# A first stage that takes x laid out transposed, in a two-layer trunk of mLSTM and retention heads

## The chip, the cores and the metric

The kernel runs on one core of a Trainium2 chip. The metric is device time in microseconds, from the start of the program to its end on that core; smaller is better. The core has five engines that run their own instruction streams in order and wait for each other by semaphores: TensorE (PE in the profile, with its weight loads listed apart as PEld), VectorE (DVE), ScalarE (ACT), GpSimd (POOL) and SyncE (SP), which here issues the transfers. TensorE reads SBUF and writes PSUM, which has eight banks of 128 partitions by 512 float32 in this kernel's use.

## The reference

Two layers; x is 1024 tokens by 1024 channels, float32. Each layer is

```
shift, scale, gate = split(silu(c) @ w_ada + b_ada, 3)          # one row each, from the condition c
h = x * rsqrt(mean(x*x, over channels) + eps) * norm_g * (1 + scale) + shift
p = h @ w_in                                                    # 1024 x 9224: gates and q, k, v of two head groups
y = concat(mLSTM heads(p), retention heads(p))                  # 4 + 4 heads of 256
x = x + gate * (y @ w_out)
```

and at the end stands one more root-mean-square norm of x. Only `h` of the first layer is computed in a different way by the change. To form it one needs, for each token, the root over its channels, and for each channel a gain `norm_g * (1 + scale)` and a shift, which come from c and a third of w_ada (two of its three column blocks; 8 MB).

## The kernel before, in words

The projections want `h` transposed: channels on partitions (eight blocks k of 128 channels), tokens along the free axis (two halves of 512). Each such tile `hT[k][half]` is kept as a pair of float32r tiles, a high part and a low part (`h` minus its high part), and each product is three matmuls: weight high by h high, weight high by h low, weight low by h high (`mm3`, lines 145 to 147).

The first stage (everything ahead of the call of `head_cols` for layer 0) makes `hT` for layer 0 and, as tiles become ready, multiplies them with the first three weight blocks (`first`, called F). It is set out by hand: a string of steps in the program, `script`, is walked in order, and each step appends its instructions to the queues of the engines it uses. No planner reorders them; within an engine the order of the string is the order of execution. The steps before are:

- the prologue: c is loaded, then eight tiles of w_ada (group 0, `ada_load`, L236), x of half 0 (L1061, eight tiles of 128 tokens by 512 channels), the first half of three weight blocks (L1076), x of half 1, w_ada groups 1 and 2, the second half of the weights, w_ada group 3, some small rows. Each tile has 256 KB. All go through SP's queue.
- `S`, `Q`, `R`: squares of x with a running sum along the free axis, half on ACT (L1072), half on DVE (L1069), then the root of each token by POOL's power (L1013), a column per 128 tokens.
- `N`, `X`: x times its token's root, a column operand (L308 on ACT, L310 on DVE).
- `A g a b`: DVE multiplies the tiles a to b of w_ada's group g with c and adds them up (L244, then L246): one group yields gain and shift of two channel blocks.
- `P g`: four one-column matmuls sum the group over its partitions (L251). `G g`: three small DVE operations turn that into gain and shift (L227, L229, L230).
- `T n`: four 128 by 128 transposes on TensorE bring one channel block of one half to PSUM (L315). `n` counts the sixteen pieces in the order: blocks 0 and 1 of half 0, blocks 0 and 1 of half 1, blocks 2 and 3 of half 0, and so on.
- `E n`: gain and shift while the block leaves PSUM (L321 on ACT, L323 on DVE). `C n`: high part (ACT, L1137). `U n`: low part (DVE, L1140).
- `F n`: nine matmuls of 512 columns, three weight blocks times high and low.
- `W i p`: a raw weight tile is split into high and low; the low part on POOL or DVE (L614, L615). `V n`: a piece of the v weights, split by ACT and POOL.
- `D n`: n matmuls on a constant (L1151).

Behind the last F comes a transpose of parameter rows (`head_cols`, L206) and then the v projection, and from there on the stages of layer 0 and 1, whose order on the other engines is chosen by a scheduler and on TensorE is fixed by the program.

Of the kernel before, what the change touches and what calls it, by code (L numbers as in the profile page):

```python
# [19 lines left out]
P = 128  # L20
# [59 lines left out]
@with_exitstack  # L80
def tile_hybrid_trunk(ctx, tc, x, c, positions, w_ada, b_ada, norm_g, w_in, conv_w, conv_b,
                      b_igate, b_fgate, gn_m, gn_r, w_out, final_g, consts, out):
# [477 lines left out]
    def ocol(hg, m):  # L560
        return OFF_MO + hg * HD + m * P
# [493 lines left out]

    def load_x(half):
        xt = [[bt() for _ in range(2)] for _ in range(4)]
        for tt in range(4):
            row = half * 4 + tt
            for cc in range(2):  # L1060
                Q.dma_start(xt[tt][cc], x[row * P:(row + 1) * P, cc * 512:(cc + 1) * 512])  # L1061
        return xt

    def squares(xt, ss, rows):
        for tt in rows:
            for cc in range(2):
                o = wt("th", 512, 5)
                if cc:
                    V.scalar_tensor_tensor(o, xt[tt][cc], 1.0, xt[tt][cc], ALU.mult, ALU.mult,  # L1069
                                           accum_out=ss[:, tt, cc:cc + 1])  # L1070
                else:
                    A.activation(o, xt[tt][cc], AF.Square, accum_out=ss[:, tt, cc:cc + 1])  # L1072

# [5 lines left out]

    xss = [new_ss(), new_ss()]  # L1080
# [12 lines left out]
    araw.append(ada_load(0, 3))  # L1093
    vgr = v0_gates(0)
# [4 lines left out]
    ada_cols(0, arows)  # L1099
    accs = [bt()]  # L1100
    ada_group(araw[0], accs[0], range(KT))
    pad = ps_a()

    for l in range(DEPTH):
# [7 lines left out]

        def first(half, k):
            for i, w in enumerate(wf):
                if k == 0:
                    pf[i][half] = ps_p() if i < 2 else ps_a()
                half_block(pf[i][half], w, hT, half, k, k + 1)

        if l == 0:
            seq = [(half, k) for g in range(4) for half in range(2) for k in (2 * g, 2 * g + 1)]  # L1120
            w0, pts, hfs, rs1 = [], {}, {}, []
            script = ("P0 D6 S G0 W00 W10 N0 W20 T0 T1 E0 E1 C0 C1 U0 U1 F0 F1 Q R A102 X0 A124 T2 E2 C2 A146 T3 D3 E3 C3 U2 F2 "
# [4 lines left out]
            for step in script.split():  # L1127
                what, arg = step[0], step[1:]
                n = int(arg) if arg.isdigit() else 0
                if what == "T":  # L1130
                    pts[n] = norm_transpose(xts[seq[n][0]], seq[n][1])
                elif what == "E":
                    hfs[n] = norm_evac(0, pts.pop(n), seq[n][1], n >= 2)
                elif what == "C":
                    half, k = seq[n]
                    hT[k][half] = (bt(F32R), bt(F32R))
                    A.copy(hT[k][half][0], hfs[n])  # L1137
                elif what == "U":
                    half, k = seq[n]
                    V.tensor_tensor(hT[k][half][1], hfs.pop(n), f(hT[k][half][0]), ALU.subtract)  # L1140
                elif what == "F":
                    first(*seq[n])
                elif what == "A":
                    g, a, b = (int(d) for d in arg)
                    if len(accs) == g:
                        accs.append(bt())
                    ada_group(araw[g], accs[g], range(a, b))
                elif what == "D":
                    warm = ps_a()
                    for i in range(n):  # L1150
                        PE.matmul(warm[:, 0:256], rmask[:, 0:P], rmask[:, 0:256], start=True, stop=True)  # L1151
                elif what == "P":
                    ada_sums(0, n, accs[n], pad)
                elif what == "G":
                    finish_gsh(0, 2 * n, 2, pad[:, 4 * n:4 * n + 2], pad[:, 4 * n + 2:4 * n + 4])
                elif what == "Q":
                    squares(xts[1], xss[1], range(4))
                elif what == "R":
                    rs1 = row_rstd(xss[1], "nrm")
                elif what == "S":  # L1160
                    squares(xts[0], xss[0], range(4))
                    rs0 = row_rstd(xss[0], "nrm")
                elif what == "N":
                    if n == 0:
                        norm_scale(xts[0], rs0, (0,), (0, 2))
                    else:
                        norm_scale(xts[0], rs0, (1,), range(4), range(2 * n - 2, 2 * n))
                elif what == "X":
                    if n == 0:
                        norm_scale(xts[1], rs1, (0,), (0, 2))  # L1170
                    else:
                        norm_scale(xts[1], rs1, (1,), range(4), range(2 * n - 2, 2 * n))
                elif what == "V":
                    w0.append(v0_split(vgr, vrw[n], n))
                    if n + 4 < KT:
                        vrw.append(v0_raw(0, n + 4))
                else:
                    i, p = (int(d) for d in arg)
                    wf[i] += split_w(rw[i][p], P, V if p else G)
# [89 lines left out]

_INS = ['x', 'c', 'positions', 'w_ada', 'b_ada', 'norm_g', 'w_in', 'conv_w', 'conv_b', 'b_igate', 'b_fgate',  # L1270
        'gn_m', 'gn_r', 'w_out', 'final_g']
# [25 lines left out]
```

## Time and profile before

| | us |
|---|---|
| median of 3 runs | 2311.9 (2310.84 to 2314.16) |
| the profiled execution | 2311.88 |
| its span, first to last instruction | 2310.0 |
| TensorE busy in the span | 2277.8 |
| start of the first F in the profile | 24.41 |
| start of L206 behind the last F | 73.96 |

A row of the timeline reads: start, duration, engine, line, operation, output and inputs by name, shapes, how many were merged into the row; in square brackets, the idle time of the engine just before it and what ended that. Where several were merged, the duration runs from the first start to the last end. A row of the table by windows has the stretch, its length, then for each engine the busy time and the number of instructions, then the clock that TensorE was granted as a share of full speed, the busy share of the transfer engines and GB/s. The chain of waits is followed back from the last instruction; in order of time its rows are start, duration, and what was being waited for or done.

### The profile page before, as it was taken

The page shows a single profiled execution, that of the slowest core. Times are in us where ns is not written, and L with a number is a line of the kernel's source. Part 1 is how long each engine was busy: PE and PEld are TensorE (multiplying, and loading weights), DVE is VectorE, ACT ScalarE, POOL GpSimd, SP SyncE. Part 2 cuts the span into 40 slices and gives each one's busy share as a digit, 9 for nine tenths or more (in the row PEclk, how much of TensorE's full clock was granted, in tenths as well). Part 3 has the DMA queues.
Part 4 walks back from the last instruction along what each step waited for, and adds up shares of the span by engine and source line. Part 5 has one row for each costly group of instructions (what it writes and reads, how often), then busy time and mean ns, then how long its engine had stood idle before and what let it go on. Part 6 is the DMA issues. An engine that isn't in the chain of part 4 may idle for free.

```text
span 2310.0 us, 34281 instructions
## 1 busy us (share of the span) xinstructions
PE 2277.8 (99%) x12447; PEld 1958.2 (85%) x12447; DVE 1353.2 (59%) x2835; ACT 907.1 (39%) x1768; POOL 823.5 (36%) x817
## 2 busy tenths in 40 slices
PE   7999999999999999999999999999999999999998
PEld 5888888889988888888888889888898888988886
DVE  7477688556555555584536665555563545556753
ACT  5535433444332323353434544344443323224442
POOL 1343424333343334222552434233334334341323
PEclk9999999999999999999999999999999999999999
DMA  8223232324433533486532322322323333436762
GB/s 257 80 64 98 73 84 80 82 74 116 120 109 88 150 83 87 128 258 217 177 92 57 84 72 77 84 74 69 81 70 89 81 87 93 124 81 205 240 231 78
DMA packets 328761, 259.44 MB, mean 112 GB/s; under 512 B 79732, under 2 KB 263804, under 8 KB 328592
## 3 DMA queue, kind: packets, MB, share of 16 engines
q1 hardware_dynamic: 328592, 257.27, 38.6%
q8 instruction: 97, 1.59, 0.3%
q14 instruction: 72, 0.59, 0.1%
HBM read 201.58 MB, written 55.61 MB: 111 GB/s over the span
## 4 chain that ended last, share of the span: by engine, by line
PE 91%; DVE 3%; DMA 3%; issue 1%; POOL 1%; ACT 1%; SPq 0%; POOLq 0%; DVEq 0%; ACTq 0%
PE pp L145 24%; PE pp L146 24%; PE pp L147 24%; PE pa L146 5%; PE pa L147 5%; PE pa L145 5%; PE pa L765 2%; DMA b<-in_w_ada_dram 1%; DMA b<-in_x_dram 1%; PE pa L315 0%; DMA raw<-in_w_ada_dram 0%; POOL wL L615 0%; POOL sL L615 0%; DVE b L266 0%; DMA b<-in_w_in_dram 0%
## 5 line engine op out<-in xcount | busy, mean ns | idle before, releaser
L145 PE MATMUL pp<-b,wH 128*128 128x512 f32 x1776 | 703.7, 396 | 1.1 <-ACT b L1137 1.1
L146 PE MATMUL pp<-b,wH 128*128 128x512 f32 x1776 | 700.2, 394 | 0.3 <-DVE b L1140 0.2
L147 PE MATMUL pp<-b,wL 128*128 128x512 f32 x1776 | 700.2, 394 | 0.0
L615 POOL TENSOR_TENSOR wL<-raw,wH 128x512 fp32r<-128x512 f32 x338 | 450.1, 1338 | 507.4 <-ACT wH L614 466.8
L147 PEld LDWEIGHTS pp<-b,wL 128*128 128x128 f32 x1776 | 333.9, 188 | 79.0
L146 PEld LDWEIGHTS pp<-b,wH 128*128 128x128 f32 x1776 | 334.2, 188 | 72.2 <-DVE b L1140 2.0
L145 PEld LDWEIGHTS pp<-b,wH 128*128 128x128 f32 x1776 | 334.4, 188 | 71.5 <-ACT b L1137 1.6
L614 ACT CAST wH<-raw 128x512 fp32r<-128x512 f32 x402 | 246.1, 616 | 322.8 <-PE pp L147 93.8
L145 PE MATMUL pp<-wH,b 128*128 128x256 f32 (+1 forms) x1152 | 353.0, 306 | 0.7 <-DVE g L543 0.7
L147 PE MATMUL pp<-wH,b 128*128 128x256 f32 (+1 forms) x1152 | 352.8, 306 | 0.0
L146 PE MATMUL pp<-wL,b 128*128 128x256 f32 (+1 forms) x1152 | 352.2, 306 | 0.0
L615 POOL TENSOR_TENSOR b<-acc,b 128x256 fp32r<-128x256 f32 (+1 forms) x208 | 200.8, 984 | 322.8 <-ACT b L614 315.2
L145 PEld LDWEIGHTS pp<-wH,b 128*128 128x128 f32 x1152 | 216.9, 188 | 12.3 <-DVE g L543 1.6
L147 PEld LDWEIGHTS pp<-wH,b 128*128 128x128 f32 x1152 | 216.6, 188 | 11.4
L146 PEld LDWEIGHTS pp<-wL,b 128*128 128x128 f32 x1152 | 216.7, 188 | 10.8
L632 DVE SCALAR_TENSOR_TENSOR acc<-pp,cols,acc 128x511 f32<-128x511 f32 (+2 forms) x192 | 142.5, 742 | 43.2 <-ACT acc L627 41.2
L614 ACT CAST b<-acc 128x256 fp32r<-128x256 f32 (+1 forms) x208 | 93.7, 487 | 187.4 <-DVE acc L709 127.6
L615 POOL TENSOR_TENSOR sL<-th,sH 128x384 fp32r<-128x384 f32 (+1 forms) x64 | 61.0, 953 | 236.5 <-ACT sH L614 171.9
L145 PE MATMUL pa<-wH,b 128*128 128x512 f32 x256 | 101.1, 395 | 0.0
L147 PE MATMUL pa<-wH,b 128*128 128x512 f32 x256 | 101.0, 394 | 0.0
L146 PE MATMUL pa<-wL,b 128*128 128x512 f32 x256 | 100.9, 394 | 0.0
L636 ACT ACTIVATE th<-acc 128x512 f32<-128x512 f32 x64 | 40.5, 632 | 146.3 <-DVE acc L634 79.3
(255 smaller groups left out, 3439.3 us busy)
## 6 DMA issues: line engine op xcount, KB each, us to landing
raw<-in_w_in_dram SPq DMA_DIRECT2D x274, 256.0 KB
raw<-in_w_out_dram SPq DMA_DIRECT2D x128, 256.0 KB
gdr<-g SPq DMA_DIRECT2D x64, 256.0 KB
ndr<-zt SPq DMA_DIRECT2D x128, 128.0 KB
raw<-in_w_ada_dram SPq DMA_DIRECT2D x64, 256.0 KB
g<-gdr SPq DMA_DIRECT2D x64, 256.0 KB
acc<-ndr SPq DMA_DIRECT2D x64, 256.0 KB
acc<-kdr SPq DMA_DIRECT2D x192, 64.0 KB
```

Of the source, the lines that this page charges most:

```text
L145: PE.matmul(o, lt[0], rt[0], start=start, stop=False)
L146: PE.matmul(o, lt[0], rt[1], start=False, stop=False)
L147: PE.matmul(o, lt[1], rt[0], start=False, stop=stop)
L614: A.copy(dst[0], src)
L615: eng.tensor_tensor(dst[1], src, f(dst[0]), ALU.subtract)
L632: V.scalar_tensor_tensor(acc[:, d:], pt[:, 0:HALF - d], wcol, acc[:, d:], ALU.mult, ALU.add)
L636: A.activation(th, acc, AF.Tanh, scale=0.5)
L765: PE.matmul(pd, kk[i][:, o:o + P], qd, start=dt == 0 and i == 0, stop=dt == 1 and i == 1)
```

## The change

The program gets a second copy of x, transposed (`xt`, channels by tokens), as an input; the first stage loads that, sixteen tiles of 128 channels by 512 tokens, and loads all of it ahead of everything but a few rows. The untransposed x is still read later for the residual. No transposes are left in the first stage, and a piece is now a tile of xt.

Since channels lie on partitions, the sum of squares of a token runs over partitions. New steps: `Z n`: ACT squares tile n (0 to 7 half 0, 8 to 15 half 1). `M n`: four matmuls with a 128 by 128 block of the squares as weights and a column of ones, each into its own bank, summed over the eight tiles of a half. `B`: four small DVE operations (L1077) and POOL's power (L1078) give the roots, token on partition. `I`/`J`: the roots times an identity, four diagonals side by side, on DVE (half 0) or POOL (half 1) (L1082). `O`: one float32 matmul of 512 columns with ones spreads them over all partitions (L1087). `R`: ACT copies that to SBUF (L1167). `X n`/`Y n`: tile n times the spread roots, on DVE or POOL (L1170). `H`: high part straight from gain and shift on ACT (L1173); `E`: the same result in full, in place (L1175); `U`/`L`: low part on DVE or POOL (L1177). `F` has its six matmuls with high parts first, then the three with low parts; this order holds in the second layer's first block too (L1131, L1132, L1134). `D n` is two matmuls that read tile n (from 16 on, a tile of w_ada's group 0). In a split, a small `w` puts the low part on DVE, a capital `W` on POOL.

```diff
-            script = ("P0 D6 S G0 W00 W10 N0 W20 T0 T1 E0 E1 C0 C1 U0 U1 F0 F1 Q R A102 X0 A124 T2 E2 C2 A146 T3 D3 E3 C3 U2 F2 "
-                      "A168 U3 P1 G1 N1 T4 F3 E4 C4 U4 N2 A202 T5 F4 E5 C5 U5 X1 A224 T6 F5 E6 C6 U6 X2 A246 T7 F6 E7 C7 "
-                      "A268 U7 W01 W11 W21 P2 G2 T8 F7 E8 C8 A302 U8 T9 F8 E9 C9 A324 U9 T10 F9 E10 C10 A346 U10 T11 F10 "
-                      "E11 C11 A368 U11 P3 G3 T12 F11 E12 C12 U12 T13 F12 V0 E13 C13 V1 U13 T14 F13 E14 C14 V2 U14 "
-                      "T15 F14 E15 C15 V3 U15 V4 F15 V5 V6 V7")
+            script = ("Z0 M0 Z1 M1 Z2 M2 Z3 M3 Z4 M4 Z5 M5 Z6 M6 Z7 M7 B0 Z8 M8 Z9 M9 I0 Z10 M10 Z11 M11 Z12 M12 O0 "
+                      "Z13 M13 Z14 M14 Z15 R0 M15 Y0 A001 B1 J1 A013 D17 D18 O1 R1 Y1 A035 D20 Y2 A057 A078 P0 w00 "
+                      "W10 G0 w20 H0 E0 A102 U0 F0 H1 E1 Y8 L1 Y9 F1 H2 E2 H3 E3 A124 L2 F2 Y3 A148 P1 G1 L3 F3 w21 "
+                      "H4 E4 H5 E5 X10 X11 L4 F4 A203 L5 W01 H6 E6 L6 W11 H7 E7 F5 A236 F6 A268 X4 P2 G2 L7 F7 H8 E8 "
+                      "Y5 H9 E9 X12 X13 L8 F8 A304 H10 E10 L9 F9 H11 E11 A348 Y6 L10 F10 P3 G3 L11 F11 H12 E12 Y7 "
+                      "U12 X14 F12 H13 E13 U13 F13 X15 H14 E14 L14 F14 V0 V1 H15 E15 U15 F15 V2 V3 V4 V5 V6 V7")
...
+    def token_squares(t):
+        o = wt("th", 512, 5)
+        A.activation(o, t, AF.Square)
+        return o
+
+    def token_sums(pt, o, start, stop):
+        for i in range(4):
+            PE.matmul(pt[i][:, 0:1], o[:, i * P:(i + 1) * P], ones, start=start, stop=stop)
+
+    def token_rstd(pt):
+        s = cst.tile([P, 4], F32, tag="nrm", bufs=2, name=nm("s"))
+        rs = cst.tile([P, 4], F32, tag="nrmr", bufs=2, name=nm("rs"))
+        for i in range(4):
+            V.tensor_scalar(s[:, i:i + 1], pt[i][:, 0:1], 1.0 / D, EPS, ALU.mult, ALU.add)
+        G.tensor_tensor(rs, s, mhalf, ALU.pow)
+        return rs
+
+    def spread_diag(dg, rs, eng=V):
+        eng.tensor_tensor(dg.rearrange("p (a b) -> p a b", a=4), ident.unsqueeze(1).to_broadcast([P, 4, P]),
+                        rs.unsqueeze(2).to_broadcast([P, 4, P]), ALU.mult)
+
+    def spread(dg):
+        pt = ps_a()
+        PE.matmul(pt, f(ones_r), dg, start=True, stop=True)
+        return pt
...
+    xh = [load_xt(half) for half in range(2)]
+    firsts = (zcol(0, 0), ocol(0, 0), zcol(0, 1))
     araw = [ada_load(0, 0)]
-    xts = [load_x(0)]
-    firsts = (zcol(0, 0), ocol(0, 0), zcol(0, 1))
     rw = [[w_raw(col, 0)] for col in firsts]
-    xts.append(load_x(1))
     araw.append(ada_load(0, 1))
-    araw.append(ada_load(0, 2))
     for i, col in enumerate(firsts):
         rw[i].append(w_raw(col, 1))
+    araw.append(ada_load(0, 2))
     araw.append(ada_load(0, 3))
...
         def first(half, k):
+            hH, hL = hT[k][half]
             for i, w in enumerate(wf):
                 if k == 0:
                     pf[i][half] = ps_p() if i < 2 else ps_a()
-                half_block(pf[i][half], w, hT, half, k, k + 1)
+                PE.matmul(pf[i][half], w[k][0], hH, start=k == 0, stop=False)
+                PE.matmul(pf[i][half], w[k][1], hH, start=False, stop=False)
+            for i, w in enumerate(wf):
+                PE.matmul(pf[i][half], w[k][0], hL, start=False, stop=k == KT - 1)
...
+                elif what in "XY":
+                    t = xh[n // 8][n % 8]
+                    (V if what == "X" else G).tensor_tensor(t, t, R[n // 8], ALU.mult)
+                elif what == "H":
+                    hT[k][half] = (bt(F32R), bt(F32R))
+                    A.activation(hT[k][half][0], src, AF.Identity, scale=gain, bias=shift)
                 elif what == "E":
-                    hfs[n] = norm_evac(0, pts.pop(n), seq[n][1], n >= 2)
+                    A.activation(src, src, AF.Identity, scale=gain, bias=shift)
+                elif what in "UL":
+                    (V if what == "U" else G).tensor_tensor(hT[k][half][1], src, f(hT[k][half][0]), ALU.subtract)
...
+                    t = xh[n // 8][n % 8] if n < 16 else araw[0][n - 16]
+                    for i in range(2):
+                        PE.matmul(warm[:, 0:256], rmask[:, 0:P], t[:, 0:256], start=True, stop=True)
```

More of the change, by code (lines that the diff above doesn't have):

```diff
@@ L1054, in tile_hybrid_trunk, with load_xt @@
     hT = [[None, None] for _ in range(KT)]
[L1056 to L1072, printed above, removed]
+    def load_xt(half):
+        tiles = []
+        for k in range(KT):
+            t = bt()
+            Q.dma_start(t, xt[k * P:(k + 1) * P, half * HALF:(half + 1) * HALF])
+            tiles.append(t)
+        return tiles
+    def token_squares(t):
[19 more added lines that the diff above has]
+        return pt
     def w_raw(col, p):
@@ L1078, in w_raw @@
         return raw
-    xss = [new_ss(), new_ss()]
     crow = wt("rows", P, 2)
@@ L1099, in tile_hybrid_trunk @@
     ada_cols(0, arows)
-    accs = [bt()]
-    ada_group(araw[0], accs[0], range(KT))
+    accs = []
     pad = ps_a()
@@ L1129, in tile_hybrid_trunk @@
                 n = int(arg) if arg.isdigit() else 0
-                if what == "T":
-                    pts[n] = norm_transpose(xts[seq[n][0]], seq[n][1])
-                elif what == "E":
-                    hfs[n] = norm_evac(0, pts.pop(n), seq[n][1], n >= 2)
[L1134 to L1140, printed above, removed]
+                if what in "HEULF":
+                    half, k = seq[n]
+                    src = xh[half][k]
+                    gain, shift = gsh[0][:, 0, k:k + 1], gsh[0][:, 1, k:k + 1]
+                if what == "Z":
+                    sqs[n] = token_squares(xh[n // 8][n % 8])
+                elif what == "M":
+                    if n % 8 == 0:
+                        sums[n // 8] = [ps_p() for _ in range(4)]
+                    token_sums(sums[n // 8], sqs.pop(n), n % 8 == 0, n % 8 == 7)
+                elif what == "B":
+                    rss[n] = token_rstd(sums[n])
+                elif what in "IJ":
+                    spread_diag(dg[n], rss[n], V if what == "I" else G)
+                elif what == "O":
+                    prs[n] = spread(dg[n])
+                elif what == "R":
+                    A.copy(R[n], prs[n])
+                elif what in "XY":
[4 more added lines that the diff above has]
+                    A.activation(hT[k][half][0], src, AF.Identity, scale=gain, bias=shift)
+                elif what == "E":
+                    A.activation(src, src, AF.Identity, scale=gain, bias=shift)
+                elif what in "UL":
+                    (V if what == "U" else G).tensor_tensor(hT[k][half][1], src, f(hT[k][half][0]), ALU.subtract)
                 elif what == "F":
-                    first(*seq[n])
+                    first(half, k)
                 elif what == "A":
```

31 lines of the change are left out of this document (7 added, 24 removed).

## The prediction

> **What bounds the kernel now.** I read the page's engine shares first, then the chain of waits, then the first 80 us on the timeline, because the change touches nothing later.
>
> ```profile
> span 2310.0 us, 34281 instructions
> PE 2277.8 (99%) x12447; PEld 1958.2 (85%) x12447; DVE 1353.2 (59%) x2835; ACT 907.1 (39%) x1768; POOL 823.5 (36%) x817
> ...
> PE 91%; DVE 3%; DMA 3%; issue 1%; POOL 1%; ACT 1%; SPq 0%; POOLq 0%; DVEq 0%; ACTq 0%
> ```
>
> TensorE carries the chain. Behind the first stage the instructions of every engine are the same in both programs, apart from a few neighbours swapped, so a later end of the first stage is a later end of the kernel. The stage's end in PE's order is the transpose of the head's rows (L206), whose start I take as the mark.
>
> ```profile
> 73.72 0.40 PE L147 MATMUL pa<-b,wL 128*128 128x512 f32 x1
> 73.96 0.25 PE L206 MATMUL pa<-ident,rows 96*128 96x96 f32 x1
> ```
>
> Up to that mark, where does the stage wait? The chain in order of time says: on transfers until 46, then on TensorE.
>
> ```profile
> 38.83 7.19 DMA b<-in_w_ada_dram
> 46.06 1.94 DMA rows<-in_conv_w_dram
> ```
>
> The weights of the conditioning arrive last. Both programs load the same 54 tiles of 256 KB through the same queue, so I let that end stay at 46 and cost the SP queue at nothing in total; only the order inside it moves. Landings read off the engines that waited for them:
>
> ```profile
> 5.08 0.49 DVE L244 TENSOR_SCALAR b<-b,cact 128x512 f32<-128x512 f32 x1 [0.96 <-DMA b<-in_w_ada_dram]
> ...
> 11.92 0.75 DVE L246 SCALAR_TENSOR_TENSOR b<-b,cact,b 128x512 f32<-128x512 f32 x1 [0.19 <-DMA b<-in_w_ada_dram]
> ```
>
> ```profile
> 12.47 0.63 ACT L1072 ACTIVATE th<-b 128x512 f32<-128x512 f32 x1 [9.25 <-DMA b<-in_x_dram]
> ...
> 18.09 0.62 ACT L614 CAST wH<-b 128x512 fp32r<-128x512 f32 x1 [0.84 <-DMA b<-in_w_in_dram]
> ```
>
> Tile 1 lands at 5.1, tile 8 at 11.9, tile 17 at 18.1. So all of x is there by about 17.5 in the new order, and the first conditioning group, tiles 17 to 24, by 18.1 + 7 x 0.75 = 23.4 (256 KB at the 350 GB/s of the windows below).
>
> **Part 1, the sums of squares on TensorE (Z, M, B, I/J, O, R).** Removed are 64 transposes. Added are 16 x 4 matmuls that load a 128x128 block of squares and move one column, the form of L251. They are f32, and the trace shows an f32 matmul as two records (L251 issues four, the row says x8; the six warm-up matmuls of L1151 are x12).
>
> ```profile
> 12.73 1.86 PE L251 MATMUL pa<-ones,b 128*128 128x1 f32 x8 [8.90 <-DVE b L246]
> ...
> 14.46 5.47 PE L1151 MATMUL pa<-rmask 128*128 128x256 f32 x12
> ...
> 24.41 0.79 PE L145 MATMUL pp<-b,wH 128*128 128x512 f32 x1 [1.12 <-ACT b L1137]
> ...
> 30.55 0.40 PE L147 MATMUL pp<-b,wL 128*128 128x512 f32 x1
> 30.79 0.39 PE L145 MATMUL pa<-b,wH 128*128 128x512 f32 x1
> ...
> 31.48 1.06 PE L315 MATMUL pa<-ident,b 128*128 128x128 f32 x8
> ...
> 36.80 0.95 PE L251 MATMUL pa<-ones,b 128*128 128x1 f32 x8
> 37.61 0.63 PE L315 MATMUL pa<-ident,b 128*128 128x128 f32 x4
> ```
>
> Removed: 64 x 1.06/8 = 8 us of TensorE. Added: 128 records. At 12.73 eight take 14.46 - 12.73 = 1.73 (0.216 each); at 36.80 eight take 37.61 - 36.80 = 0.81 (0.101 each). The sums cost 27.7 or 13.0, by the clock. Which?
>
> ```profile
> 13.41:16.83 3.42, 3.42 (x12) 2.97 (x13) 1.81 (x6) 1.75 (x5) 0.00 (x0) 1.00 1.07 385
> 16.83:20.24 3.41, 3.09 (x8) 1.92 (x6) 2.00 (x8) 2.28 (x6) 1.73 (x2) 1.00 1.13 334
> 20.24:23.65 3.41, 1.53 (x8) 0.87 (x8) 2.99 (x4) 1.17 (x3) 3.35 (x3) 0.96 1.05 393
> 23.65:27.07 3.42, 2.66 (x6) 1.84 (x7) 3.39 (x9) 3.23 (x9) 0.00 (x0) 0.50 1.08 366
> 27.07:30.48 3.41, 3.41 (x10) 2.69 (x9) 2.86 (x9) 0.68 (x3) 1.19 (x1) 0.54 1.10 350
> ```
>
> These windows (length, then busy time and count of PE, PEld, DVE, ACT, POOL, then granted clock) are cut where the clock changes: full from 20.24, half from 23.65, full from 30.48. Before 20.24 no clock is recorded and the column shows 1.00; the pitch, 0.456 a record in the warm-up, shows half speed. In 13.41 to 16.83 PE was busy throughout, 1 us of it with one-column sums, and the clock stayed low; one window filled almost wholly with wide matmuls (16.83 to 20.24, and again 27.07 to 30.48) raised it. I take it that one-column sums don't count as work, and price all of them at 0.216. The other reading, that the rise comes one window late whatever fills it, stays as a rival.
>
> The Trainium skill, "TensorE: Matmul & The Clock Gate", section "Part 1: The HAM clock gate", states that about 4 us of sustained matmul activity lift the array to full clock. By that, the sums, unbroken from 5.8, would be at full clock from about 10; the two rises here came 6 us after the first wide matmul, and no row shows sums alone.
>
> Place by place: the first square ends at 5.1 + 0.6; the sums run from 5.8 without a break, since 1.73 a piece is slower than the landings; the roots of half 0 (four small reads of the banks that the next sums need) add 0.5 (0.16 each, as L227 below); the spreading product O0 stands among the sums and is f32 of 512 columns, 4 x 0.456 = 1.8. The last sum ends at 5.8 + 27.7 + 0.5 + 1.8 = 35.8. B1 on DVE waits for it, and behind B1 in DVE's order are seven of the eight multiply-adds of the first conditioning group, whose data landed long before. After B1: 36.3. The warm-ups D17, D18, D20 (4 x 0.456 each) and O1 follow on PE until 35.8 + 7.3 = 43.1 and are covered by what comes next on DVE.
>
> **Part 2, the moves to POOL.** The scaling by the token root becomes 16 products of two tensors (7 on DVE, 9 on POOL); of the 16 low parts 12 go to POOL; three weight splits and one diagonal are there too. That is 25 operations of 128x512 with two SBUF inputs on POOL, where this stage had 3 (and the small v splits at its end). What does such an operation do to a DVE one with two SBUF inputs?
>
> ```profile
> 19.50 4.09 POOL L615 TENSOR_TENSOR wL<-b,wH 128x512 fp32r<-128x512 f32 x3
> ```
>
> ```profile
> 563.11 1.29 POOL L615 TENSOR_TENSOR wL<-raw,wH 128x512 fp32r<-128x512 f32 x1
> 563.29 1.65 DVE L266 SCALAR_TENSOR_TENSOR b<-raw,cact,b 128x512 f32<-128x512 f32 x1 [0.64 <-DMA raw<-in_w_ada_dram]
> ...
> 564.35 1.74 POOL L615 TENSOR_TENSOR wL<-raw,wH 128x512 fp32r<-128x512 f32 x1
> 564.98 1.67 DVE L266 SCALAR_TENSOR_TENSOR b<-raw,cact,b 128x512 f32<-128x512 f32 x1
> ```
>
> ```profile
> 28.88 0.48 DVE L244 TENSOR_SCALAR b<-b,cact 128x512 f32<-128x512 f32 x1
> 29.39 0.75 DVE L246 SCALAR_TENSOR_TENSOR b<-b,cact,b 128x512 f32<-128x512 f32 x1
> ...
> 31.07 3.11 DVE L246 SCALAR_TENSOR_TENSOR b<-b,cact,b 128x512 f32<-128x512 f32 x4
> ...
> 37.78 0.16 DVE L227 TENSOR_TENSOR gsh<-pa,cols 128x2 f32<-128x2 f32 x1 [0.94 <-PE pa L251]
> ...
> 38.04 0.16 DVE L230 TENSOR_TENSOR gsh<-sm,cols 128x2 f32<-128x2 f32 x1
> ...
> 49.12 1.89 DVE L615 TENSOR_TENSOR wL<-b,wH 128x512 fp32r<-128x512 f32 x3
> ```
>
> They take turns. Alone the DVE form takes 0.75, four of them 3.11 (pitch 0.79); beside POOL each ends 0.55 after the POOL operation does (563.11 + 1.29 = 564.40, DVE ends at 564.94), and the POOL operation after it is held as well (1.74). POOL ends at 564.40 and 566.09, so a pair takes 1.69, and a POOL operation that meets a busy DVE costs DVE 1.69 - 0.79 = 0.9. The bounds are 0 (POOL always elsewhere in time) and 1.29 (the whole operation).
>
> The Trainium skill, "SBUF — State Buffer", section "SBUF: two separate sides", states that the port pair shared by DVE and GpSimd is an exclusive lock held for the whole instruction. The trace agrees that they alternate; taken at the full 1.29 for 23 operations the sum would be 23 x 0.39 = 9 us more.
>
> DVE's order has, per conditioning group: eight multiply-adds, then G waits for P on PE, which waits for the eighth, and the next group stands behind G. From the rows: P and G together are 38.20 - 36.80 + 0.1 = 1.5. DVE's own work between G's, at pitches of 0.60 (a split, a low part or a product, as the three at 49.12), 0.51 (L244, 28.88 to 29.39) and 0.79 (L246), and the POOL operations that meet it by the two orders:
> - to P0: 7 x 0.79 = 5.5, and dg1, Y1, Y2, W10, Y8: 5 x 0.9. From 36.3: 46.3.
> - G0 to G1: 2 x 0.60 + 0.51 + 7 x 0.79 = 7.2, and L1, Y9, L2, Y3, L3: 4.5. With 1.5: 13.2.
> - G1 to G2: 3 x 0.60 + 6.0 = 7.8, and L4, L5, W01, L6, W11, L7, Y5: 6.3. With 1.5: 15.6.
> - G2 to G3: 2 x 0.60 + 6.0 = 7.2, and L8, L9, Y6, L10, L11, Y7: 5.4. With 1.5: 14.1.
>
> P0 follows a pause of PE, so I take its slow row: 46.3 + 1.86 + 0.55 = 48.7 for G0. F0 starts one H (below) later, at 49.4 (24.41 before). G3: 48.7 + 13.2 + 15.6 + 14.1 = 91.6. TensorE needs 36 x 0.232 + 0.8 = 9.2 a group and is not the limit there: it waits at P1, P2 and P3, where P stands ahead of an F that could run.
>
> **Part 3, behind G3.** F11 stands behind P3 (done at 91.2), then F12 to F15: 45 matmuls at 0.232 (30.79 after 30.55, rounded) are 10.4. PE paused for some 4 us before P3, so it may restart at half clock (0.43) for one or two windows: 1.7 to 3.4, taken as 2.5. U12 and U15 add 0.5. Mark: 104.6, against 73.96: +31.
>
> Edits at nothing. ACT's H and E:
>
> ```profile
> 39.63 1.33 ACT L308 ACTIVATE b<-b,rs 128x512 f32<-128x512 f32 x2
> ```
>
> Two are 1.33, so a piece's pair is done before POOL's part for the piece ahead (1.69); without that cover, at most one piece, 1.3. POOL's splits of the v weights follow L14 and feed the product behind the mark: 0 to 2.5 late, kept in the range. In the second layer the low parts come after the high ones, 64 records swapped; TensorE is busy throughout there, so nothing.
>
> Sum: 2311.9 + 31 = 2343; the profiled execution took 2311.9 (span 2310.0), which is the median of the runs.
>
> **The rivals.**
> (a) The sums do raise the clock. For: the late-rise reading of 13.41 to 20.24, and the skill's rule. Then they end at 5.8 + 3 x 1.73 + 13 x 0.81 + 0.5 + 0.9 = 22.9 (three pieces slow), everything behind is 12.9 earlier: mark at 92, +18, 2330.
> (b) DVE and POOL don't collide, the sums are slow. For: POOL waits for ACT often. Against: by both orders POOL has work ready in each group. DVE is done at 41.8, PE's warm-ups at 43.1, P0 and G0 2.4 and H: F0 at 46.2, then 144 x 0.232 + 3 x 0.8 + 2.5: mark at 84.5, +10, 2322.
> (c) Faster: TensorE is again the only limit of the stage, with 8 us of transposes and pauses gone. It decides from F0 at 38 on, since 144 x 0.232 + 3 x 0.8 = 36 lie between it and the mark: earlier is faster. With F0 at 31 (sums as in (a), B1 0.5, first group 5.5, P0 to F0 2.1): 67, -7, 2305. For: DMA allows it, the first group lands at 23.4. Against: the 0.216 and the 1.69.
>
> **How the numbers follow.** (The runs tell no change from about 0.2%, 4.6 us.) Forecast 0.46, (a) 0.25, (b) 0.12, (c) 0.12, within 0.2% (between (b) and (c)) 0.05. Slower 0.83, same 0.05, faster 0.12. Alone the forecast lies in 2336 to 2350 (collisions at 0.7 to 1.1 each, restart 1.7 to 3.4, v splits up to 2.5). The range leaves out (c) and no change below, and the top: 2317 to 2348.
>
> **What would show it.** Right: sums at 0.21 a record, the last near 36; B1 followed by an unbroken run of L246 at 1.7 apart beside POOL; F0 near 49; PE idle ahead of P1, P2, P3 with DVE L246 as releaser. Wrong: sums at 0.10 with the clock full by 13; L246 at 0.75 while POOL runs; PE without a pause from F0 on; or ada3 landing later than 46.

## The result and the profile after

The changed kernel took 2340.25 us (median of 4 runs, 2338.49 to 2341.04) against 2311.66 (4 runs): a ratio of 1.0121, 95% interval 1.0103 to 1.0138. It is slower by 28.6 us; the forecast was 2343. The profiled execution took 2340.62, its span is 28.9 longer. The page of the changed kernel:

```profile
span 2338.9 us, 34415 instructions
PE 2303.9 (99%) x12509; PEld 1982.9 (85%) x12509; DVE 1358.6 (58%) x2813; ACT 908.6 (39%) x1760; POOL 858.8 (37%) x839
```

The shares hardly tell the two kernels apart; the first 102 us do. The timeline of TensorE in the changed kernel (start, duration, line, operation, operands, records, and in brackets the idle time ahead and what ended it):

```profile
5.61 22.35 PE L1071 MATMUL pp<-ones,th 128*128 128x1 f32 x104 [1.73 <-ACT th L1066]
27.82 2.05 PE L1087 MATMUL pa<-g,ones_r 128*128 128x512 f32 x2
29.67 5.12 PE L1071 MATMUL pp<-ones,th 128*128 128x1 f32 x24
34.65 3.76 PE L1189 MATMUL pa<-b,rmask 128*128 128x256 f32 x8
...
43.85 1.84 PE L251 MATMUL pa<-ones,b 128*128 128x1 f32 x8 [2.98 <-DVE b L246]
47.11 0.80 PE L1131 MATMUL pp<-b,wH 128*128 128x512 f32 x1 [1.42 <-ACT b L1173]
...
56.90 1.05 PE L251 MATMUL pa<-ones,b 128*128 128x1 f32 x8 [0.44 <-DVE b L246]
...
72.51 1.87 PE L251 MATMUL pa<-ones,b 128*128 128x1 f32 x8 [4.60 <-DVE b L246]
...
87.46 1.87 PE L251 MATMUL pa<-ones,b 128*128 128x1 f32 x8 [2.94 <-DVE b L246]
...
102.11 0.25 PE L206 MATMUL pa<-ident,rows 96*128 96x96 f32 x1
```

The sums (L1071), with the spreading product O0 (L1087) among them, hold TensorE without a break until 34.8; F0 (the first L1131) starts at 47.11 (24.41 before); TensorE waits for VectorE's multiply-adds (L246) ahead of all four P (L251); the mark, L206, is at 102.11, 28.15 later than the 73.96 of before. All but half a us of the 28.6 stands ahead of the mark.

VectorE and GpSimd in the changed kernel, from the same timeline; L230 ends a G:

```profile
34.91 8.80 DVE L246 SCALAR_TENSOR_TENSOR b<-b,cact,b 128x512 f32<-128x512 f32 x7
...
45.99 0.16 DVE L230 TENSOR_TENSOR gsh<-sm,cols 128x2 f32<-128x2 f32 x1
...
58.26 0.16 DVE L230 TENSOR_TENSOR gsh<-sm,cols 128x2 f32<-128x2 f32 x1
...
60.67 11.79 DVE L246 SCALAR_TENSOR_TENSOR b<-b,cact,b 128x512 f32<-128x512 f32 x7
63.44 1.76 POOL L615 TENSOR_TENSOR wL<-b,wH 128x512 fp32r<-128x512 f32 x1
65.14 1.75 POOL L1177 TENSOR_TENSOR b<-b,b 128x512 fp32r<-128x512 f32 x1
66.85 1.72 POOL L615 TENSOR_TENSOR wL<-b,wH 128x512 fp32r<-128x512 f32 x1
...
74.68 0.16 DVE L230 TENSOR_TENSOR gsh<-sm,cols 128x2 f32<-128x2 f32 x1
...
89.62 0.16 DVE L230 TENSOR_TENSOR gsh<-sm,cols 128x2 f32<-128x2 f32 x1
```

Seven multiply-adds take 11.79, 1.68 each, while GpSimd's operations start 1.70 apart. Alone they take 0.75. The two engines take turns, as forecast.

In the runs below the mark moves by what the stage gains or loses. It is read in the one execution that was profiled, and the total is the median of all; against the kernel before, the median moved between 2 us less and 5 us more than the mark. So mechanisms are read at the mark, the totals stand beside it, and a total that hits its forecast within 5 us shows little by itself. All in us; the ratio is to the kernel before:

| kernel | F0 | G3 done | mark | median | ratio (95%) |
|---|---|---|---|---|---|
| before | 24.41 | 62.04 | 73.96 | 2311.66 | |
| changed | 47.11 | 89.78 | 102.11 | 2340.25 | 1.0121 (1.0103 to 1.0138) |
| all on VectorE | 47.85 | 85.20 | 95.17 | 2336.93 | 1.0108 (1.0093 to 1.0123) |
| first group first | 44.89 | 89.89 | 101.48 | 2342.14 | 1.0131 (1.0116 to 1.0146) |
| one record a sum | 35.75 | 78.44 | 90.72 | 2327.28 | 1.0066 (1.0049 to 1.0083) |
| warm-ups first | 47.45 | 89.30 | 100.91 | 2343.35 | 1.0133 (1.0118 to 1.0148) |
| first group free | 38.38 | 84.14 | 94.17 | 2335.40 | 1.0099 (1.0085 to 1.0113) |
| before, x first | 34.08 | 72.76 | 84.63 | 2320.58 | 1.0036 (1.0022 to 1.0049) |
| rearranged | 29.48 | 62.88 | 72.87 | 2312.41 | 1.0002 (0.9992 to 1.0011) |
| two tiles on TensorE | 29.11 | 65.52 | 75.87 | 2315.43 | 1.0012 (1.0003 to 1.0021) |
| rearranged, full sums | 40.35 | 73.72 | 83.69 | 2323.44 | 1.0050 (1.0032 to 1.0068) |

### The profile page after: what moved, and what is told of

The parts are those of the page before. It is cut to its first block, busy times and chain, and to the rows that moved or that the text cites. A ratio compares the mean times of both kernels' runs of the same rounds, so it can differ in the third digit from the quotient of the medians.

```text
span 2338.9 us, 34415 instructions
## 1 busy us (share of the span) xinstructions
PE 2303.9 (99%) x12509; PEld 1982.9 (85%) x12509; DVE 1358.6 (58%) x2813; ACT 908.6 (39%) x1760; POOL 858.8 (37%) x839
## 5 line engine op out<-in xcount | busy, mean ns | idle before, releaser
L146 PE MATMUL pp<-b,wH 128*128 128x512 f32 x1712 | 675.0, 394 | 0.0
L145 PE MATMUL pp<-b,wH 128*128 128x512 f32 x1712 | 674.5, 394 | 0.0
L147 PE MATMUL pp<-b,wL 128*128 128x512 f32 x1712 | 674.5, 394 | 0.0
L147 PEld LDWEIGHTS pp<-b,wL 128*128 128x128 f32 x1712 | 321.5, 188 | 75.1
L145 PEld LDWEIGHTS pp<-b,wH 128*128 128x128 f32 x1712 | 321.7, 188 | 68.5
L146 PEld LDWEIGHTS pp<-b,wH 128*128 128x128 f32 x1712 | 321.6, 188 | 68.2
L146 PEld LDWEIGHTS pp<-wL,b 128*128 128x128 f32 x1152 | 216.7, 188 | 10.7
```

Source lines behind the costliest of these rows:

```text
L145: PE.matmul(o, lt[0], rt[0], start=start, stop=False)
L146: PE.matmul(o, lt[0], rt[1], start=False, stop=False)
L147: PE.matmul(o, lt[1], rt[0], start=False, stop=stop)
```

## The experiments

**All products and low parts on VectorE: do the two engines collide?** The letters Y, L and J of the order (GpSimd) become X, U and I (VectorE), at the same places.

```diff
-"... M15 Y0 A001 B1 J1 A013 ... Y8 L1 Y9 F1 ... Y6 L10 F10 P3 G3 L11 F11 ..."
+"... M15 X0 A001 B1 I1 A013 ... X8 U1 X9 F1 ... X6 U10 F10 P3 G3 U11 F11 ..."
```

> The 9 products, 12 low parts and one diagonal that the change gave to GpSimd go to VectorE, at the same places of the order; only three weight splits stay on GpSimd. Theory (each GpSimd operation with two SBUF inputs costs a busy VectorE 0.9 us, since the two take turns): each of the 22 costs VectorE 0.60 instead of 0.9. Ahead of G0 four of them are in the way, between G0 and G1 five, G1 and G2 five, G2 and G3 six: G0 1.2 earlier (44.5), G0 to G1 10.8 (12.3 in the changed kernel), G1 to G2 14.9 (16.4), G2 to G3 13.1 (14.9); together 6 us, 2334. Rival (the two do not collide, VectorE is slow there for another reason): VectorE gets 22 x 0.60 = 13 us more to do, 2353. A multiply-add that stands with none of the three splits beside it takes 0.79 by the theory, still over 1.2 by the rival.

The mark came 6.9 earlier (95.17). The groups by line and form, of the changed kernel between 60.6 and 72.5 us and of this one between 50 and 85 (after the bar: busy us, mean ns of one, idle us ahead):

```profile
L246 DVE SCALAR_TENSOR_TENSOR b<-b,cact,b 128x512 f32<-128x512 f32 x7 | 11.6, 1653 | 0.2
```

```profile
L246 DVE SCALAR_TENSOR_TENSOR b<-b,cact,b 128x512 f32<-128x512 f32 x20 | 15.9, 796 | 0.6
```

The multiply-add takes 796 ns with GpSimd nearly empty (two of its operations are left in those 35 us) and 1653 beside a busy one. VectorE was given 13 us more work, and the stage ended 6.9 earlier: the rival (2353) is out. From G0 on the intervals are 11.8, 13.6 and 12.85 (10.8, 14.9 and 13.1 expected, 12.3, 16.4 and 14.9 in the changed kernel); G0 itself came 0.8 later (44.5 expected): the sums ended 0.65 later, and the products ahead of it are now VectorE's. Not all of the 6.9 is VectorE's time: 4.6 stand at G3 (85.20 against 89.78), and 1.7 of these come from P2 and P3, which ran at 1.05 and 0.95 in place of 1.87 each; the other 2.3 come behind G3, where TensorE needed 10.0 at full clock in place of 12.3.

```profile
70.84 1.05 PE L251 MATMUL pa<-ones,b 128*128 128x1 f32 x8 [2.46 <-DVE b L246]
...
83.80 0.95 PE L251 MATMUL pa<-ones,b 128*128 128x1 f32 x8
```

In the total 3.3 of the 6.9 are left. TensorE's order behind the mark is the same in both kernels, and the difference shrinks from 7.2 at 1210 us to 4.7 at 2155; why is open.

**The first conditioning group ahead of B1: what does the wait behind the sums cost?**

```diff
-"... M15 Y0 A001 B1 J1 A013 D17 D18 O1 R1 Y1 A035 D20 Y2 A057 A078 P0 w00 W10 G0 w20 H0 E0 ..."
+"... M15 Y0 A008 P0 B1 G0 J1 D17 D18 O1 R1 Y1 D20 Y2 w00 W10 w20 H0 E0 ..."
```

> The first conditioning group's eight multiply-adds, its sums P0 and its G0 are put ahead of B1's part of the order. Theory (B1, waiting for the last sum, holds up multiply-adds whose data landed by 23): they run while TensorE does the sums, P0 stands right behind the last sum, G0 is done near 37.2 (45.7 to 46.15 in the changed kernel), F0 near 39 (47.1). The GpSimd operations that met A0 (the diagonal, Y1, Y2, W10: 3.6 us) now meet the second group, so G0 to G1 grows from 12.3 to about 16: G1 near 53.5 (58.0), and the gain that lasts is some 4.5 us: 2336. Rival 1 (the order alone counts, all 8.5 us last): 2332. Rival 2 (something else sets the end, the late start is hidden): G3 stays at 89.4, 2340.

The group was done at 27.5 and G0 at 37.3, as expected, but F0 came only at 44.89, and the mark stayed (101.48). The timeline of this kernel shows a new wait in the place of the one removed:

```profile
36.48 3.76 PE L1189 MATMUL pa<-b,rmask 128*128 128x256 f32 x8
40.03 1.92 PE L1087 MATMUL pa<-g,ones_r 128*128 128x512 f32 x2
41.98 0.59 ACT L1167 COPY g<-pa 128x512 f32<-128x512 f32 x1 [11.36 <-PE pa L1087]
43.12 0.69 DVE L615 TENSOR_TENSOR wL<-b,wH 128x512 fp32r<-128x512 f32 x1 [5.78 <-ACT wH L614]
```

ScalarE stands at R1 (L1167) for the spreading product O1, which stands on TensorE behind warm-ups (L1189) that had been hidden so far; the casts of the weight splits, and H0, are queued behind R1, and VectorE idles 5.8 behind those. The expectation had not looked at ScalarE's order.

**The same, with those three things out of the way.**

```diff
+"... M15 Y0 A008 P0 w00 W10 w20 B1 G0 J1 H0 E0 O1 R1 Y1 Y2 A102 U0 F0 ..."
```

> As the run with the first conditioning group ahead of B1, and three things besides that stood in the way there: the warm-ups D17, D18, D20 are left out, the three weight splits come ahead of B1, and H0, E0 ahead of the copy R1 in ScalarE's order. Theory (what held F0 at 44.9 in that run was ScalarE waiting at R1 for O1, which stood behind cold warm-ups on TensorE; the collisions of GpSimd and VectorE are still to be paid): G0 done near 37.2, F0 near 38.5, 8.6 earlier than in the changed kernel. Ahead of G1 stand 6.6 of VectorE's own work, 1.5 for P1 and G1, and now nine GpSimd operations (the diagonal, Y1, Y2, Y8, L1, Y9, L2, Y3, L3) x 0.9 = 8.1: G1 near 53.4 (58.0), G2 16.4 and G3 31.3 later, G3 near 84.7 (89.4), mark 97.4 (102.1): 2335.6. Rival 1 (the start alone counts): all of 8.6 lasts, mark 93.5, 2332. Rival 2 (something else sets the end): mark near 101.5 as in the first run, 2341.

```profile
36.84 0.42 DVE L230 TENSOR_TENSOR gsh<-sm,cols 128x2 f32<-128x2 f32 x1
38.38 1.42 PE L1131 MATMUL pp<-b,wH 128*128 128x512 f32 x1
...
53.60 0.16 DVE L230 TENSOR_TENSOR gsh<-sm,cols 128x2 f32<-128x2 f32 x1
...
69.86 0.16 DVE L230 TENSOR_TENSOR gsh<-sm,cols 128x2 f32<-128x2 f32 x1
...
83.98 0.16 DVE L230 TENSOR_TENSOR gsh<-sm,cols 128x2 f32<-128x2 f32 x1
```

F0 at 38.38, G1 at 53.8 (53.4 expected), G3 at 84.1 (84.7). F0 gained 8.7, and by G1 only 4.7 of it is left: GpSimd's operations that had met the first group now meet the second. At the mark 7.9 are left, 3.2 more than expected, 2.3 of it gained behind G3: TensorE needed 10.0 from there to the mark instead of 12.3, at full clock (from 74.97 on in this trace, where the changed kernel runs at half clock from 87.41 to 94.24). The profiled execution is 7.8 faster than the changed kernel's, the median only 4.9; that the median, 2335.4, meets the 2335.6 expected is luck.

**One record a sum: is it the number of short matmuls?** The squares are rounded to float32r, and the sums read them so; that changes their precision.

```diff
-        o = wt("th", 512, 5)
+        o = wt("th", 512, 5, F32R)
...
-            PE.matmul(pt[i][:, 0:1], o[:, i * P:(i + 1) * P], ones, start=start, stop=stop)
+            PE.matmul(pt[i][:, 0:2], o[:, i * P:(i + 1) * P], ones_r[:, 0:2], start=start, stop=stop)
```

> The squares are written in the rounded 32-bit type and the sums read them in it, so each sum is one record (of two columns) in place of two: 64 records for 128. The sums lose some precision. Theory (sums run at the cold price whatever their number, 0.216 each): a piece takes 0.87, the last sum ends at 5.8 + 64 x 0.216 + 0.5 + 1.8 = 21.9, if the squares keep up (the last of x lands near 17.5), against 34.8. B1 is then over before the first group's last tile lands, near 23.4; with the collisions that group ends near 31, 12 us earlier than the 43.7, and G0, F0, G1, G2, G3 and the mark all follow: 2328. Rival (the one-column sums are hidden, the work of VectorE and GpSimd sets the end from elsewhere): under 4 us, 2337 or more. If a record of the rounded type takes as long as two of the other, nothing changes.

```profile
9.61 9.55 PE L1071 MATMUL pp<-ones_r,th 128*128 128x2 f32 x44 [2.07 <-ACT th L1066]
19.01 2.05 PE L1087 MATMUL pa<-g,ones_r 128*128 128x512 f32 x2
20.08 3.34 PE L1071 MATMUL pp<-ones_r,th 128*128 128x2 f32 x12
...
78.28 0.16 DVE L230 TENSOR_TENSOR gsh<-sm,cols 128x2 f32<-128x2 f32 x1
...
90.72 0.25 PE L206 MATMUL pa<-ident,rows 96*128 96x96 f32 x1
```

A record still takes 0.214 ((19.01 - 9.61)/44), the last sum ends at 23.4, and everything behind it comes 11.4 earlier: G0 34.8, G3 78.4, mark 90.72. On the four other engines this kernel's order is the changed kernel's, so this is the cleanest of the runs. The intervals between the G's are those of the changed kernel (12.3, 16.4, 15.0): they belong to VectorE and GpSimd, not to the sums.

**Warm-ups ahead of the sums: can a raised clock be kept?**

```diff
+                elif what == "K":
+                    warm = ps_a()
+                    for i in range(n):
+                        PE.matmul(warm[:, 0:256], rmask[:, 0:P], rmask[:, 0:256], start=True, stop=True)
-            script = ("Z0 M0 Z1 M1 ...
+            script = ("K10 Z0 M0 Z1 M1 ...
```

> Ten wide warm-up matmuls (20 records, 0.456 each cold) stand ahead of the first sum, with nothing to wait for but the mask: they fill TensorE from about 2.5 to 10 or 11.6, so that the clock is full when the sums start. Theory (one-column sums do not count as work for the clock): it falls again one or two windows of 3.4 us later; 34 to 68 sums at 0.101, the rest at 0.216, so that the last ends between 32 and 38; 2337 to 2343. Rival (sums keep a raised clock up; only the start from cold was the trouble): 128 x 0.101 = 13 from 11.6, the last ends near 27, B1 8 us earlier: 2332.

Windows of this kernel, cut where its clock changes (length, then busy us and count of PE, PEld, DVE, ACT, POOL, then granted clock; ahead of 6.99 none is recorded and the column shows 1.00):

```profile
3.58:6.99 3.41, 3.33 (x8) 2.70 (x9) 0.26 (x2) 0.96 (x2) 0.00 (x0) 1.00 0.84 278
6.99:13.82 6.83, 6.83 (x51) 6.47 (x49) 0.00 (x0) 4.37 (x8) 0.00 (x0) 1.00 1.01 376
13.82:27.50 13.68, 13.68 (x66) 13.68 (x65) 1.72 (x6) 4.75 (x8) 1.02 (x1) 0.50 1.11 352
```

One 3.4 us stretch filled with wide matmuls raises the clock at 6.99. The sums begin at 9.82, with the clock full; after a stretch of 3.4 us with nothing but sums, TensorE busy throughout, it falls to half at 13.82 and stays there for 27.3 us. The sums in full clock (some 37, which start 0.112 apart) nearly paid for the 4.2 us that the warm-ups put ahead of them: the last one ends at 35.2 against 34.8. The rival is out: short sums neither raise the clock nor keep it. The total, 2343.35, is at the top of what was expected; the mark is 1.2 earlier than the changed kernel's, so what was lost arose behind it. At like records of TensorE the profiled execution is 1.2 ahead of the changed kernel's at the mark and 0.7 behind it after 3.4 us more at half clock (from 106 to 109); at 600 us it is 2.9 behind, and why is open.

The Trainium skill, "TensorE: Matmul & The Clock Gate", section "Part 1: The HAM clock gate", says that a busy window of about 3.4 us lifts the array to full clock and an idle one lets it fall. The traces agree on the length (3.41) for wide matmuls. For f32 matmuls of one column they do not: 29 us of them, with TensorE marked busy throughout, left it at half clock: the pitch of 0.214 stands where half clock is recorded in this run (13.82 to 27.50), and all through the sums of the changed kernel.

**The load order alone, in the kernel before.**

```diff
-    araw = [ada_load(0, 0)]
-    xts = [load_x(0)]
+    xts = [load_x(0), load_x(1)]
+    araw = [ada_load(0, 0)]
...
-    xts.append(load_x(1))
```

> The kernel before with one part of the change alone: all of x is loaded ahead of the first conditioning group. Theory (the load order costs, since the group's last tile lands near 23.4 instead of 11.9): its multiply-adds end near 24.2 instead of 12.7, VectorE's half of the squares, which stands behind them, at 27.4 instead of 18.0, and F0 comes near 34 instead of 24.4; of those 9.5 us up to 4 are taken up by slack ahead of the last group, whose data lands at 46 either way: 5.5 to 9.5 later at the mark, 2317 to 2321. Rival (the stage waits for the last landing anyway): no change, 2312.

```profile
19.05 5.48 DVE L246 SCALAR_TENSOR_TENSOR b<-b,cact,b 128x512 f32<-128x512 f32 x7 [0.27 <-DMA b<-in_w_ada_dram]
...
34.08 0.50 PE L145 MATMUL pp<-b,wH 128*128 128x512 f32 x1 [1.12 <-ACT b L1136]
...
84.63 0.25 PE L206 MATMUL pa<-ident,rows 96*128 96x96 f32 x1
```

F0 at 34.08, as expected; no slack took any of it up, the mark is 10.7 later, the median 8.1 and the profiled execution 12.0. In the changed kernel this cost is hidden: the first group was complete at 27.4 (in the two runs that put it first), and the sums last until 34.8. With short sums it should come out: in the rearranged kernel below, VectorE waits 1.60 for the first tile of that group (18.22). What the old load order would give there was not tried.

**Everything at once: is there a version that is level?** Sums of one record; products, low parts and splits on VectorE; the first group as it lands; each P between two F's; the multiply-adds of a group spread so that VectorE has one at hand while ScalarE makes the next pair.

```diff
+"... Z10 M10 Z11 O0 M11 Z12 M12 Z13 R0 M13 Z14 M14 Z15 M15 A002 X0 A024 X1 A046 B1 A068 I1 D17 P0 O1 w00 w10 w20 G0
+ H0 E0 H1 E1 R1 A103 U0 F0 A134 U1 F1 X8 X9 H2 E2 H3 E3 A147 U2 F2 A178 P1 U3 F3 X2 X3 G1 ..."
```

A first form of it:

> The changed kernel with every cause found so far taken away: sums of one record each (rounded squares), products, low parts and weight splits all on VectorE, the products X0, X1 while the first group lands, that group ahead of or around B1, each P behind an F that can run and followed by one, no warm-ups but one. Theory (TensorE is again the stage's limit if F0 starts early enough, and a start at 38 is as good as the kernel before): the sums end near 23.5, the first group near 26.5, P0 28.4, F0 near 31; VectorE has some 38 us of its own work behind it, TensorE 36: mark near 69 to 71 against 73.96, 2307 to 2310. Rival (VectorE's own work, 13 us more than in the kernel before, still sets the end, or the cold clock eats the start): mark at 74 or later, 2312 or more.

Its order left out one multiply-add of the second group, so its output is not the reference's. F0 came at 28.75, but the mark at 82.31, 2323.6: ahead of G1 VectorE stood 5.1 for a transfer of w_ada, which the next run, with the tile read, does not show. The form without the slip:

> The rearranged kernel of the run before, now with the multiply-add of the second group that its order left out by mistake, and with the multiply-adds of a group spread so that VectorE has one to do while it waits for ScalarE. Theory (VectorE's own work is what is left: 6.0 for a group, 2.4 for four low parts, 2.4 for four products, 1.8 for the splits in one of them, and the wait of 5.1 for a transfer of that run was the left-out tile's): G0 near 27.9, G1 near 39.5, G2 53.5, G3 66, and from there 10 to the mark: 76, 2314. TensorE idles 2 to 3 us a group. Rival (TensorE is the limit once nothing collides): F0 at 29 plus 36, mark near 67, 2305.

```profile
28.41 0.16 DVE L230 TENSOR_TENSOR gsh<-sm,cols 128x2 f32<-128x2 f32 x1
29.48 0.79 PE L1131 MATMUL pp<-b,wH 128*128 128x512 f32 x1
...
62.72 0.16 DVE L230 TENSOR_TENSOR gsh<-sm,cols 128x2 f32<-128x2 f32 x1
...
72.87 0.25 PE L206 MATMUL pa<-ident,rows 96*128 96x96 f32 x1
```

```profile
28.60:39.40 10.80, 10.78 (x42) 7.84 (x41) 10.56 (x20) 6.80 (x9) 0.00 (x0) 1.00 1.11 347
39.40:52.10 12.70, 11.75 (x49) 8.76 (x48) 12.47 (x24) 7.90 (x12) 0.00 (x0) 0.90 0.67 199
52.10:62.90 10.80, 9.81 (x43) 6.86 (x42) 10.56 (x20) 6.32 (x8) 0.00 (x0) 0.96 0.01 2
```

Level with the kernel before: 2312.41, ratio 1.0002 (0.9992 to 1.0011); the mark is 1.1 earlier. The windows, cut at the G's, show VectorE busy 10.56 of 10.80, 12.47 of 12.70 and 10.56 of 10.80: it has no time left, and TensorE, at 10.78, 11.75 and 9.81, hardly any. The intervals, 10.8, 12.6 and 10.8, came out 0.8 to 1.7 us shorter than expected; they are VectorE's own work at the prices of the expectation (6.0 + 2.4 + 2.4, and 1.8 for the splits), with nothing left for the wait at P and G. The squares are rounded in this kernel, as in the one-record run, so it is level at a lower precision of the sums.

**Work from VectorE to TensorE.** Two of the eight tiles of each later group are read by TensorE itself, against the conditioning column.

```diff
-    def ada_sums(l, g, acc, pt):
+    def ada_sums(l, g, acc, pt, more=()):
+        parts = [(acc, ones)] + [(raw, cact[:, kk:kk + 1]) for raw, kk in more]
...
+                for n, (a, v) in enumerate(parts):
+                    PE.matmul(... a[:, which * 256 + i * P:which * 256 + (i + 1) * P], v,
+                              start=n == 0, stop=n == len(parts) - 1)
```

> The same, with two of the eight multiply-adds of each of the last three groups left to TensorE: it reads the two raw tiles as weights against the conditioning column in place of ones, eight short matmuls more a group (16 records, 1.6 at full clock). Theory (VectorE is the limit of that kernel, TensorE has 2 to 3 us a group to spare): VectorE loses 1.6 a group; G1 near 38, G2 50.5, G3 61.5, mark near 72: 2310, within 0.2% of the kernel before. Rival (the two engines wait for one another at each G, so that work moved from one to the other gains nothing): mark as without it, near 76, 2314.

```profile
28.00:40.00 12.00, 11.98 (x54) 9.27 (x52) 9.14 (x16) 6.80 (x9) 0.00 (x0) 0.98 1.11 347
40.00:52.00 12.00, 12.00 (x58) 10.03 (x57) 11.08 (x20) 7.88 (x11) 0.00 (x0) 0.88 0.64 188
52.00:64.00 12.00, 12.00 (x57) 10.01 (x56) 9.45 (x18) 6.33 (x8) 0.00 (x0) 0.86 0.01 2
```

The mark is 3.0 later than without it, 75.87, and so is the median, 2315.43, with ranges that overlap (2312.96 to 2317.45, and 2310.65 to 2314.48). VectorE now has idle time, TensorE has none, and its clock falls to half for 3.4 us at the end of P1 (39.55) and again 0.8 behind P2 (53.21). In the rearranged kernel it falls once, at 49.56. The expectation had counted 2 to 3 us a group to spare on TensorE, from a kernel that still had waits; the rearranged one had 0.02 to 1.0.

**The rearranged kernel with full sums.** The two lines of the one-record run are put back, nothing else.

> The rearranged kernel, which was level with the kernel before, with one thing put back: the squares and their sums in full float32, two records each. Theory (sums cold at 0.216 a record, VectorE's own work behind them): the last sum ends near 35 as in the changed kernel, the warm-up and P0 cold behind it 1.8 and 1.9, G0 near 39.2 against 28.6, F0 near 40.6; from G0 on the intervals of the rearranged kernel (34.3 to G3, 10.2 from there to the mark): mark near 84 against 72.9, 2323. Rival (the prediction's third rival: a first F at 38 is as good as the kernel before, because TensorE's 36 us are all that lies behind it): mark near 77, 2315.

```profile
40.35 0.80 PE L1131 MATMUL pp<-b,wH 128*128 128x512 f32 x1
...
83.69 0.25 PE L206 MATMUL pa<-ident,rows 96*128 96x96 f32 x1
```

F0 40.35 (40.6 expected), mark 83.69 (84), 2323.44 (2323). The sums in full float32 cost 10.8 at the mark here and 11.4 in the changed kernel's own order. So of the 29.2 us between the changed kernel and the rearranged one (102.11 to 72.87) 10.8 are the sums and 18.4 the rest. Taken alone, GpSimd's share was 6.9 and the start of the order 7.9; the 3.6 that the two miss of 18.4 are the later part of the order, or what the changes do to one another; neither was tried alone.

## Why the prediction was right, and where its terms were off

*Part 1, the sums.* Right in price and place: 128 records at 0.214 ((27.82 - 5.61)/104), 27.3 in all (27.7), last sum at 34.8 (35.8 forecast). The reading of the clock from two rows of the kernel before held, and the warm-ups-first run shows it directly. Rival (a), 2330, is out with it: even a clock raised on purpose did not last, and at full clock a record takes 0.112 (that run), not the 0.101 of the forecast.

*B1 ahead of the first group.* The wait was there and named. What it would be worth to take it away was not said, and the first attempt gained nothing at the mark: the wait went over to O1, R1 and the casts. Only with those gone did F0 move by 8.7.

*Part 2, the collisions.* The price of 0.9 held: pairs were 1.70 apart (1.69 forecast). The number of meetings was too high at first and the price of P too low later:
- to G0: the seven multiply-adds took 8.80, not 10.0, and began 1.4 earlier (34.9), so G0 ended at 46.15 (48.7);
- G0 to G1 12.3 (13.2): GpSimd waited for ScalarE's pairs, which start 1.56 apart where 1.33 had been taken, and met less;
- G1 to G2 16.4 (15.6), G2 to G3 14.9 (14.1): I had taken P at its warm price; behind waits of 4.60 and 2.94 it ran cold, 1.87 instead of 1.05, which is the 0.8 in each.

The errors nearly cancel, which is luck: G0 to G3 took 43.6, 42.9 forecast. Rival (b), no collisions, is out by the all-on-VectorE run.

The Trainium skill, "SBUF — State Buffer", section "SBUF: two separate sides", has the port pair that VectorE and GpSimd share locked for a whole instruction. The traces agree on the taking of turns, not on the whole price: 1.29 and 0.79 alone are 1.70 together, so 0.4 of a pair overlaps. By the full 1.29 the all-on-VectorE run would have gained 20 x (1.29 - 0.60) = 13.8 us up to G3; by 0.9 it is 6.0. Measured there were 4.6, 1.7 of them from P at full clock, so not every one of the operations had met a busy VectorE. The 6.9 at the mark lies near the 6 us expected by luck, since the clock of TensorE gave more than half of it.

*Part 3.* From G3 to the mark 12.3 (13.0 forecast), the restart at half clock included. The v splits were late: TensorE waited 1.1 for them behind the mark (0 to 2.5 forecast).

*Rival (c), the faster side.* Its mechanism was wrong as well as its chance: a first F at 38 would not have been enough. With F0 at 38.4, 40.4 and 29.5 the mark stood 55.8, 43.3 and 43.4 behind it, never 36. What was left out is VectorE's own work, 10.6 to 12.5 us a group in the windows of the rearranged kernel, where TensorE had been given 9.2 (it was busy 9.8 to 11.75 there, part of that at half clock). To be level, the change needs F0 near 30 (73.96 - 43.4), which takes the short sums, the products and low parts off GpSimd, and an order that keeps VectorE filled.

*The sum.* The mark came 2.5 earlier than forecast (102.11, 104.6): 2.55 at G0, less 0.7 in the intervals, 0.7 behind G3, within rounding. That is about the distance between 2343 and 2340.25.

*Edits at nothing.* The load order was hidden by the sums, as said, and costs 10.7 at the mark where nothing hides it. The second layer's changed order cost nothing that shows: at like records ahead of that block (1000 us) and behind it (1500 us) the two kernels stand 30.1 and 29.9 apart. At the mark it is 28.2, at 128 us 30.2 and at 2155 us 29.2.

## What to carry to other kernels

Price a short matmul by the clock that stands there, and ask whether the work itself counts for the clock: the 128 records of the one-column sums were 27.3 us here, and ten warm-ups ahead of them gained nothing (the last sum ended at 35.2 against 34.8). Before work goes to a second engine to relieve a first, look for a row where both read two operands at once: an operation of 1.3 us on GpSimd cost VectorE 0.9, where doing it itself cost 0.6. And when a wait is taken away, read what is queued behind the next one on every engine, before counting the gain.

## What the runs showed of the hardware

- Short matmuls lower a raised clock while TensorE is marked busy all the time: one 3.4 us stretch of sums was enough (at 13.82 in the warm-ups-first run). In the two-tiles run, a P of 24 short records took 2.7 to 2.9 us, and the clock fell to half behind two of the three. The stretches of 3.41 us that end where it fell (36.14 to 39.55, 49.80 to 53.21) held 2.4 and 2.6 us of P; counted on in such steps, the third P lies in two stretches, with 1.1 and 1.5 us. Whether the few columns or the float32 form makes the difference was not tried.
- A float32r matmul of two columns is one record and takes as long as one record of the two of a float32 matmul of one column: 0.214 both. For the float32 form half clock is recorded with that pitch (the warm-ups-first run); for the other no clock is recorded.
- ScalarE's pairs with scale and bias columns start 1.56 apart, and one takes 1.65 from its first start to its last end (H and E, in the rows below from the changed kernel, with the start of the next pair), where the pair with a scale alone took 1.33 so measured in the kernel before. In the rearranged kernel VectorE waits 2.3 in all for E.

```profile
47.81 0.80 ACT L1173 ACTIVATE b<-b,gsh 128x512 fp32r<-128x512 f32 x1
48.65 0.81 ACT L1175 ACTIVATE b<-b,gsh 128x512 f32<-128x512 f32 x1
49.37 0.80 ACT L1173 ACTIVATE b<-b,gsh 128x512 fp32r<-128x512 f32 x1
```
